# Sums of the expert outputs in three groups, other pages for expert weights, and the next block's first loads put last

## The chip, the cores and the metric

The kernel runs on one core of a Trainium2 chip. The metric is the device time of one execution in microseconds; three runs of the kernel before gave 3153.24, 3155.69 and 3157.79, median 3155.69. The core has a matrix engine (TensorE, PE in the rows, its weight loads PEld), VectorE (DVE), ScalarE (ACT), GpSimd (POOL) and SyncE (SP), which here issues nearly all DMAs from one queue, in order.

## The reference

Two transformer blocks over 512 tokens of width 1024, all in float32. The change lies in the mixture of experts of the first block and the entry of the second:

```
g_sel = argmax(x @ w_group + b_group)                 # 4 groups of 8 experts
e_top, e_loc = top_k(expert logits of the group, 2)   # 2 of 32 experts per token
hid = silu(xb @ w1[e]) * (xb @ w3[e])                 # 1024 -> 512, per expert e
ys  = hid @ w2[e]                                     # 512 -> 1024
out = segment_sum(ys * gate, token)                   # back to the tokens
h   = rmsnorm(h + g2 * out) * final_g
# block 2:
x   = layer_norm(h, ln_in_g, ln_in_b);  proj = x @ w_in[0]; ...
```

## The kernel before

**Expert stage.** The 32 experts are taken in 16 pairs; the two experts of a pair use 64 columns of TensorE's array each (`both`, L1368), so a matmul has tile `128*64`. Pair j does:

- `pair_in` (L1373): tokens times w1 and w3 of both experts. The weights come as 16 loads of 512 KB, each [128, 2, 512], and are used as float32 as they land (`w` in the rows, results `e`).
- `pair_tokens` (L1357): eight transposes (`xgt`) of the next pair's gathered tokens. `pair_gather` (L1354) is an indirect DMA from GpSimd, two pairs ahead.
- `pair_loads` and `pair_out` (L1390, L1400) for pair j-1: eight loads of 512 KB of w2 (`w2r`), four transposes of the hidden values (`hdt`), a copy (`hp`), then the matmuls.
- `outputs` (L1282): gate and scale (`y`), a split in two float32r parts (`yh`, `yl`), then eight sums over the tokens (`combine`, L1295). Each sum is two matmuls of tile `128*128` into a bank (`cmb`) and one addition into `h` on VectorE (L1303). `combine` is a generator, `beside`; the call of `pair_in` two pairs later advances it once after each of its eight pieces.

**What sets the order.** The code is written as dataflow on tiles; a scheduler with its own cost model puts the instructions of each engine in a fixed order, and an engine then keeps to it. A tile takes a page of its tag, and a load waits until the page's last reader is done: 24 pages PG (4 KB in each partition), 3 WH and 3 WL (4 KB), 3 RAW (8 KB), 3 banks for `trp`. In the pairs w1 and w3 use PG for their first two pieces, WH for the third, WL for the fourth; w2 uses PG. RAW, WH and WL are also used by `expert_in` and `expert_out` (L1318, L1333), inside a branch (`more`, L1423) for experts with more than 64 tokens. The branch's body does not run with these inputs, but a page that it uses is not loaded ahead of it for later use.

**Entry of block 2.** At j = 16 (L1460) three rows (`fgR`, `lng`, `lnb`, 512 KB each in the tile) and the first weights of block 2 (`nav_weights`, L1414: two RAW loads of 1024 KB, which `prepare` splits on ScalarE and VectorE into `wh`, `wl`) are asked for ahead of `pair_loads(15)`.

Of the kernel before, what the change touches and what calls it, by code (L numbers as in the profile page):

```python
# [10 lines left out]
F32 = mybir.dt.float32  # L11
# [53 lines left out]
def build(ctx, tc, I, out, dbg=None):  # L65
# [10 lines left out]
    def t_(shape, dt, tag, name):  # L76
        uid[0] += 1
        return sb.tile(shape, dt, tag=tag, bufs=NB[tag], name=f"{name}_{uid[0]}")
# [18 lines left out]
    def pipelined(n, score, out, steps=4):  # L97

        late = None
        for h in range(n + 1):
            for i in range(steps):
                if h < n:
                    score(h, i)
                if h:
                    products = out(h - 1, i)
                    rest = late and late()
                    late = products
                    if rest:  # L110
                        late = lambda a=rest, b=products: (a(), b())[1]
                yield
        while late:
            late = late()

    def sg(name, w=512, dt=F32):
        return t_([128, w], dt, "SG", name)
# [20 lines left out]
    def split(hi, lo, src, eng=None):  # L138
        S.copy(hi, src)  # L139
        (eng or V).tensor_tensor(lo, src, f(hi), OP.subtract)  # L140
# [144 lines left out]
    def mm3(ps, l, r, start, stop):  # L285

        mmk(ps, [(l, r)], start, stop)
# [35 lines left out]
    class FM:  # L323


        def __init__(self, W, xs, base, end, eng=None):
            self.eng = eng
            self.W, self.xs, self.base, self.end = W, xs, base, end
            self.kgs = groups(len(xs), 8)
            self.cur = -1  # L330
# [42 lines left out]
    class TM:  # L373
# [1 line left out]

        def __init__(self, kt, W, c0, n, name="tm", lead=0, tail=0):
            self.kt, self.W, self.c0, self.n, self.name, self.lead, self.tail = kt, W, c0, n, name, lead, tail
            gr = 2048 // n  # L380
            raws = [(k, min(gr, kt - k)) for k in range(0, kt, gr)] if n == 512 else groups(kt, gr)
            self.pieces = [(k0, k1, g1) for k0, g in raws for k1, g1 in groups(g, 1024 // n)]
            self.size = dict(raws)
            self.raw = {}
            for p in self.pieces[:lead]:
                self.fetch(p[0])
            self.first = None

        def fetch(self, k0):
            n, g = self.n, self.size[k0]  # L390
            if k0 not in self.raw:
                self.raw[k0] = t_([128, g, n], F32, "RAW", "raw")
                load(self.raw[k0], self.W[k0 * 128:(k0 + g) * 128, self.c0:self.c0 + n].rearrange("(k p) n -> p k n", p=128))
            return self.raw[k0]

        def piece(self, p, page=None):
# [580 lines left out]
    def row(name, src, pinned=False):  # L977
        t = pg(name, F32, (128, 1024))
        ins = load(t, src.partition_broadcast(128))
        if pinned:  # L980
            tc.keep_in_program_order(ins)
        return t
# [272 lines left out]
    def rows_of(t):  # L1255
        return lambda i: t[i * 128:(i + 1) * 128, :]
# [25 lines left out]
    def outputs(py, gtc, rows):  # L1282

        place = sa("place", 512, F32R)
        V.tensor_tensor(place.rearrange("p (i n) -> p i n", n=128), iota[:, 0:128].unsqueeze(1).to_broadcast([128, 4, 128]),
                        rows.unsqueeze(2).to_broadcast([128, 4, 128]), OP.is_equal)
        y = pt_("y", F32, (128, 1024))
        yh = pt_("yh", F32R, (128, 1024))
        yl = pt_("yl", F32R, (128, 1024))
        for m in range(2):  # L1290
            cs = slice(m * 512, m * 512 + 512)
            V.scalar_tensor_tensor(y[:, cs], py[m], gtc, g2R[:, cs], OP.mult, OP.mult)  # L1292
            split(yh[:, cs], yl[:, cs], y[:, cs])

        def combine():  # L1295
            for i in range(4):
                for m in range(2):
                    cs = slice(m * 512, m * 512 + 512)
                    ps = trp("cmb")
                    pl = place[:, i * 128:(i + 1) * 128]  # L1300
                    PE.matmul(ps, pl, yl[:, cs], start=True, stop=False)  # L1301
                    PE.matmul(ps, pl, yh[:, cs], start=False, stop=True)  # L1302
                    V.tensor_tensor(h1[i][m], h1[i][m], ps, OP.add)  # L1303
                    yield
        return combine()

    def tokens(tokc, xg):
        gather(tokc, xg)
# [9 lines left out]
    def expert_in(W1, W3, xh, xl):  # L1318
        pss = []
        for W in (W1, W3):  # L1320
            ps = mmp("e1")
            for q in range(4):
                raw = t_([128, 2, 512], F32, "RAW", "w13")
                load(raw, W[q * 256:(q + 1) * 256, :].rearrange("(k p) n -> p k n", p=128))
                hi = t_([128, 2, 512], F32R, "WH", "wh")
                lo = t_([128, 2, 512], F32R, "WL", "wl")
                split(hi, lo, raw)
                mmk(ps, [((xh[:, 2 * q + k], xl[:, 2 * q + k]), (hi[:, k], lo[:, k])) for k in range(2)],
                    q == 0, q == 3)
            pss.append(ps)  # L1330
        return hidden(*pss)

    def expert_out(hd, W2):  # L1333
        b = trp("hdt")
        for k in range(4):
            PE.transpose(b[:, k * 128:(k + 1) * 128], hd[:, k * 128:(k + 1) * 128], ident)
        hp = pt_("hp")
        split(hp[:, 0], hp[:, 1], b)
        py = [mmp("e2") for _ in range(2)]
        for k in range(4):  # L1340
            raw = t_([128, 1024], F32, "RAW", "w2r")
            load(raw, W2[k * 128:(k + 1) * 128, :])
            hi = t_([128, 1024], F32R, "WH", "wh")
            lo = t_([128, 1024], F32R, "WL", "wl")
            split(hi, lo, raw)
            for m in range(2):
                cs = slice(m * 512, m * 512 + 512)
                ks = slice(k * 128, k * 128 + 128)
                mm3(py[m], (hp[:, 0, ks], hp[:, 1, ks]), (hi[:, cs], lo[:, cs]), k == 0, k == 3)
        return py  # L1350


# [15 lines left out]
    def both(ps, lhs, rhs, start, stop):  # L1368
        for h in range(2):
            hs = slice(CAP * h, CAP * h + CAP)  # L1370
            PE.matmul(ps[hs], lhs[:, hs], rhs[h], start=start, stop=stop)  # L1371

    def pair_in(j, xT, beside):  # L1373
        pss = []
        for nm in ("moe_w1", "moe_w3"):
            W = [I[nm][0, 2 * j + h].rearrange("(p a) n -> p a n", a=8) for h in range(2)]
            ps = mmp("e1")
            for q in range(4):
                ws = []
                for h in range(2):  # L1380
                    raw = t_([128, 2, 512], F32, ("PG", "PG", "WH", "WL")[q], "w13")
                    load(raw, W[h][:, 2 * q:2 * q + 2])
                    ws.append(raw)
                for k in range(2):
                    both(ps, xT[:, 2 * q + k], [w[:, k] for w in ws], q + k == 0, q + k == 4)
                next(beside, None)
            pss.append(ps)
        return hidden(*pss)

# [10 lines left out]
    def pair_out(j, hd, ws):  # L1400
        b = trp("hdt")
        cols = hd.rearrange("p (a j) -> p j a", j=4)
        for k in range(4):
            PE.transpose(b[:, k * 128:(k + 1) * 128], cols[:, k], ident)
        hp = sg("hp")
        S.copy(hp, b)
        py = [mmp("e2") for _ in range(2)]
        for k in range(4):
            for m in range(2):
                cs = slice(m * 512, m * 512 + 512)  # L1410
                both(py[m], hp[:, k * 128:k * 128 + 128], [w[:, cs] for w in ws[2 * k:2 * k + 2]], k == 0, k == 3)
        return outputs(py, gt0[:, j:j + 1], rows0[:, :, j])

    def nav_weights(l):  # L1414
        return TM(8, I["w_in_2"][l], 1024, 512, "nav", lead=3)

    g2R = row("g2R", mod_d[3])
    xres = [dr.tile([512, 1024], F32, name=f"xres{n}") for n in range(4)]
# [24 lines left out]
    rows0 = const("rows0", [128, 4, 16])  # L1443
    token_rows(tok0, rows0)
    nav_tm = None
    beside = iter(())
    prev = None
    pair_gather(0)
    more(CAP)
# [2 lines left out]
    for j in range(17):  # L1452
        hd = None
        if j < 16:
            hd = pair_in(j, xs, beside)
        if j < 15:
            xs = pair_tokens(j + 1)
        if j < 14:
            pair_gather(j + 2)
        if j == 16:  # L1460
            fgR = row("fgR", I["final_g"])
            norm, xT = normalizer(I["ln_in_g_2"], I["ln_in_b_2"], rows_of(xres[0]))
            nav_tm = nav_weights(0).prepare()
        if prev is not None:
            for _ in beside:
                pass
            beside = pair_out(j - 1, prev, pair_loads(j - 1))
        prev = hd
    for _ in beside:
        pass  # L1470
# [507 lines left out]
```

## Time and profile before

| | |
|---|---|
| median of 3 runs | 3155.69 us |
| profiled execution | 3154.16 us, its span 3152.4 us |
| PE busy | 2970.1 us, 94% of the span |
| DVE / ACT / POOL busy | 1848.6 / 1131.5 / 279.6 us |
| HBM read | 486.50 MB |
| expert stage, first to last `e` matmul | 664.5 to 1205 us |

A row of the chain of waits is a piece of the path that ended last: start, length, engine, tile, line. A window row gives a stretch, the busy time of each engine, PE's granted clock (1.00 is full), the busy share of the 16 DMA engines and the GB/s that they moved. Times of rows are microseconds from the start of the span.

### The profile page before, as it was taken

To read this page: it belongs to the slowest core of one execution; us is meant where nothing else is said; L and a number is where in the kernel's file an instruction comes from. 1 tells how busy PE (TensorE), PEld (TensorE's weight loads), DVE (VectorE), ACT (ScalarE), POOL (GpSimd) and SP (SyncE) were. 2 spreads that over 40 slices of the span, in tenths; PEclk is the share of its full clock that TensorE was granted. 3 is DMA by queue.
4 is the path that set the end of the run, shared out by engine and by line. 5 is a ranking of instruction groups with operands and counts; after the bars stand their busy time and mean duration, and the time that the engine had idled before them with its cause. 6 is when DMAs were issued, how large, how long until landed. Compare 5 with 4: busy or idle time off the path is not lost.

```text
span 3152.4 us, 36476 instructions
## 1 busy us (share of the span) xinstructions
PE 2970.1 (94%) x13749; PEld 2204.3 (70%) x13749; DVE 1848.6 (59%) x3521; ACT 1131.5 (36%) x1986; POOL 279.6 (9%) x263
## 2 busy tenths in 40 slices
PE   6988999979999998999999999999999999999998
PEld 5766777733333335878867788888888876788887
DVE  6899888633223227555589754434545588764434
ACT  4555244210000003444567332222444576432221
POOL 2133000300000000221000200000221000200000
PEclk9989999989999999999999999999999999999999
DMA  6222756679999995432233623243433234632341
GB/s 222 92 90 65 233 185 195 208 289 353 362 372 377 358 376 193 137 114 94 76 112 111 231 100 107 92 142 100 147 117 101 79 99 116 225 107 93 107 139 62
DMA packets 296257, 534.17 MB, mean 169 GB/s; under 512 B 30279, under 2 KB 172789, under 8 KB 296071
## 3 DMA queue, kind: packets, MB, share of 16 engines
q1 hardware_dynamic: 293480, 527.46, 48.5%
q0 software_dynamic: 2304, 4.20, 0.5%
q8 instruction: 110, 1.80, 0.2%
q14 instruction: 77, 0.62, 0.1%
q10 hardware_dynamic: 286, 0.09, 0.0%
HBM read 486.50 MB, written 44.38 MB: 168 GB/s over the span
## 4 chain that ended last, share of the span: by engine, by line
PE 64%; DVE 7%; issue 3%; DMA 2%; ACT 2%; POOL 1%; SPq 0%; DVEq 0%; POOLq 0%; ACTq 0%
PE e L1371 12%; PE fm L292 9%; PE fm L295 9%; PE fm L293 9%; PE ffo L295 2%; PE ffo L293 2%; PE ffo L292 2%; PE cmb L1301 1%; PE cmb L1302 1%; POOL tl L1634 1%; DVE xT L140 1%; DMA w2r<-in_moe_w_dram 1%; PE mix L292 1%; PE mix L295 1%; PE mix L293 1%
## 5 line engine op out<-in xcount | busy, mean ns | idle before, releaser
L140 DVE TENSOR_TENSOR wl<-raw,wh 128x1024 fp32r<-128x1024 f32 (+3 forms) x403 | 462.3, 1149 | 313.8 <-ACT wh L139 312.2
L139 ACT CAST wh<-raw 128x1024 fp32r<-128x1024 f32 (+3 forms) x403 | 388.6, 966 | 543.0 <-PE fm L295 224.2
L292 PE MATMUL fm<-xT,wh 128*128 128x512 f32 (+1 forms) x1264 | 481.9, 384 | 0.0
L293 PE MATMUL fm<-xT,wl 128*128 128x512 f32 (+1 forms) x1264 | 479.9, 382 | 1.3 <-DVE wl L140 1.3
L295 PE MATMUL fm<-xT,wh 128*128 128x512 f32 (+1 forms) x1264 | 301.9, 381 | 0.0
L1371 PE MATMUL e<-w,xx 128*64 128x512 f32 x1024 | 293.8, 605 | 0.0
L293 PEld LDWEIGHTS fm<-xT,wl 128*128 128x128 f32 x1264 | 238.2, 188 | 46.7 <-DVE wl L140 1.7
L292 PEld LDWEIGHTS fm<-xT,wh 128*128 128x128 f32 x1264 | 238.2, 189 | 45.1
L295 PEld LDWEIGHTS fm<-xT,wh 128*128 128x128 f32 x1264 | 231.6, 188 | 45.5
L1371 PEld LDWEIGHTS e<-w,xx 128*64 128x64 f32 x1024 | 79.2, 137 | 138.6 <-issue 130.0
L293 PE MATMUL fm<-uT,wl 128*128 128x512 f32 (+1 forms) x360 | 145.3, 403 | 3.8 <-DVE wl L140 3.8
L1303 DVE TENSOR_TENSOR h<-h,cmb 128x512 f32<-128x512 f32 x128 | 84.6, 686 | 109.2 <-PE cmb L1302 108.5
L1371 PE MATMUL e<-w2r,hp 128*64 128x512 f32 x512 | 141.9, 607 | 3.6 <-DMA w2r<-in_moe_w_dram 2.1
L292 PE MATMUL fm<-uT,wh 128*128 128x512 f32 (+1 forms) x360 | 145.0, 404 | 0.0
L292 PE MATMUL ffo<-wl,hid 128*128 128x512 f32 x352 | 137.1, 390 | 0.0
L293 PE MATMUL ffo<-wh,hid 128*128 128x512 f32 x352 | 136.9, 389 | 0.0
L1371 PEld LDWEIGHTS e<-w2r,hp 128*64 128x64 f32 x512 | 52.8, 137 | 87.9 <-issue 64.5
L1921 DVE SCALAR_TENSOR_TENSOR ffs<-ffs,fm 128x512 f32<-128x512 f32 x44 | 30.3, 688 | 137.7 <-ACT ffs L1920 137.7
L295 PE MATMUL ffo<-wh,hid 128*128 128x512 f32 x352 | 108.4, 389 | 0.0
L139 ACT CAST yh<-y 128x512 fp32r<-128x512 f32 x32 | 19.8, 618 | 224.2 <-DVE y L1292 224.2
L1923 DVE SCALAR_TENSOR_TENSOR ffs<-ffs,fm 128x512 f32<-128x512 f32 x44 | 30.3, 688 | 114.4 <-PE fm L295 114.4
L1634 POOL TENSOR_TENSOR tl<-ml,tl 128x512 f32<-128x512 f32 x32 | 47.7, 1497 | 554.3 <-DVE tl L1630 540.6
(603 smaller groups left out, 5955.6 us busy)
## 6 DMA issues: line engine op xcount, KB each, us to landing
w<-in_moe_w_dram SPq DMA_DIRECT2D x256, 512.0 KB
raw<-in_w_in_dram SPq DMA_DIRECT2D x71, 1024.0 KB
w2r<-in_moe_w_dram SPq DMA_DIRECT2D x128, 512.0 KB
raw<-in_w_ffn_in_dram SPq DMA_DIRECT2D x44, 1024.0 KB
raw<-in_w_mod_dram SPq DMA_DIRECT2D x42, 512.0 KB
raw<-in_w_ffn_out_dram SPq DMA_DIRECT2D x20, 1024.0 KB
raw<-in_w_out_dram SPq DMA_DIRECT2D x12, 1024.0 KB
t_d<-bg SPq DMA_DIRECT2D x48, 256.0 KB
```

The lines of the kernel that those rows point to most:

```text
L139: S.copy(hi, src)
L140: (eng or V).tensor_tensor(lo, src, f(hi), OP.subtract)
L292: PE.matmul(ps, l[0], r[1], start=start and n == 0, stop=False)
L293: PE.matmul(ps, l[1], r[0], start=False, stop=False)
L295: PE.matmul(ps, l[0], r[0], start=False, stop=stop and n == len(pairs) - 1)
L1301: PE.matmul(ps, pl, yl[:, cs], start=True, stop=False)
L1302: PE.matmul(ps, pl, yh[:, cs], start=False, stop=True)
L1303: V.tensor_tensor(h1[i][m], h1[i][m], ps, OP.add)
L1371: PE.matmul(ps[hs], lhs[:, hs], rhs[h], start=start, stop=stop)
L1634: G.tensor_tensor(th, m, th, OP.add)
L1921: V.scalar_tensor_tensor(s, s, 1.0, pgt, OP.add, OP.mult)
L1923: V.scalar_tensor_tensor(s, s, 0.5, pup, OP.mult, OP.mult)
```

## The change

- `behind(ins, first)` makes an instruction stand behind another of its engine. `pair_in` hands the last matmul of a piece to `combine`, and the first sum of a group is put behind it. The eight sums come in groups of 3, 3 and 2 instead of one per piece.
- The pieces of w1 are 4, 2 and 2 long on RAW, PG, PG; of w3 2, 2, 2, 2 on PG, PG, WH, WL. So a pair has two loads of 1024 KB (8 KB in a row of HBM) and twelve of 512 KB for w1 and w3.
- `expert_in` and `expert_out` take their weights in halves through small pages (`sg`, `sa`) and no longer use RAW.
- At j = 16 the rows and the first weights of block 2 are asked for behind `pair_loads(15)`, kept in program order, and `prepare` is called behind `pair_out`.

```diff
+    def behind(ins, first):
+        tc.add_manual_dep(ins.ins, first.ins.name, mybir.DependencyInfo(mybir.DependencyClass.NoSync, mybir.DependencyReason.DATA),
+                          reason="order")
+        return ins
...
         def combine():
+            after = yield
             for i in range(4):
                 for m in range(2):
...
-                    PE.matmul(ps, pl, yl[:, cs], start=True, stop=False)
+                    mm = PE.matmul(ps, pl, yl[:, cs], start=True, stop=False)
+                    if after is not None:
+                        behind(mm, after)
                     PE.matmul(ps, pl, yh[:, cs], start=False, stop=True)
                     V.tensor_tensor(h1[i][m], h1[i][m], ps, OP.add)
-                    yield
+                    after = yield
...
-            for q in range(4):
+            k = 0
+            for tag, w, banks in ((("RAW", 4, 0), ("PG", 2, 3), ("PG", 2, 0)), (("PG", 2, 3), ("PG", 2, 0), ("WH", 2, 2), ("WL", 2, 0)))[n]:
                 ws = []
                 for h in range(2):
-                    raw = t_([128, 2, 512], F32, ("PG", "PG", "WH", "WL")[q], "w13")
-                    load(raw, W[h][:, 2 * q:2 * q + 2])
+                    raw = t_([128, w, 512], F32, tag, "w13")
+                    load(raw, W[h][:, k:k + w])
                     ws.append(raw)
-                for k in range(2):
-                    both(ps, xT[:, 2 * q + k], [w[:, k] for w in ws], q + k == 0, q + k == 4)
-                next(beside, None)
+                for m in range(w):
+                    mm = both(ps, xT[:, k + m], [r[:, m] for r in ws], k + m == 0, k + m == 7)
+                k += w
+                if beside:
+                    for b in range(banks):
+                        try:
+                            beside.send(None if b else mm)
+                        except StopIteration:
+                            pass
...
-        if j == 16:
-            fgR = row("fgR", I["final_g"])
-            norm, xT = normalizer(I["ln_in_g_2"], I["ln_in_b_2"], rows_of(xres[0]))
-            nav_tm = nav_weights(0).prepare()
...
-            beside = pair_out(j - 1, prev, pair_loads(j - 1))
+            ws = pair_loads(j - 1)
+            if j == 16:
+                fgR = row("fgR", I["final_g"], True)
+                norm, xT = normalizer(I["ln_in_g_2"], I["ln_in_b_2"], rows_of(xres[0]))
+                nav_tm = nav_weights(0, True)
+            beside = pair_out(j - 1, prev, ws)
+            if j == 16:
+                nav_tm.prepare()
```

TensorE's order at the end of w2 and the start of a later pair's w1, in a middle pair, before (`e` with `w` are w1 and w3, `cmb` the sums; the trace records two matmuls for each `e` row):

```order
L1371 MATMUL e_1487_7324<-w_1488_7325,xx_7256 64x512
L1301 MATMUL cmb_7333<-yl_7317,place_7313 128x512
L1302 MATMUL cmb_7333<-yh_7316,place_7313 128x512
L1301 MATMUL cmb_7345<-yl_7317,place_7313 128x512
L1371 MATMUL e_1487_7324<-w_1489_7327,xx_7256 64x512
L1371 MATMUL e_1487_7324<-w_1488_7325,xx_7256 64x512
L1371 MATMUL e_1487_7324<-w_1489_7327,xx_7256 64x512
L1302 MATMUL cmb_7345<-yh_7316,place_7313 128x512
L1301 MATMUL cmb_7357<-yl_7317,place_7313 128x512
L1302 MATMUL cmb_7357<-yh_7316,place_7313 128x512
```

The same place now, from the last of the twelve `e` rows that stand between w2 and the first group:

```order
L1385 MATMUL e_1527_7500<-w_1531_7515,xx_7432 64x512
L1311 MATMUL cmb_7521<-yl_7493,place_7489 128x512
L1314 MATMUL cmb_7521<-yh_7492,place_7489 128x512
L1311 MATMUL cmb_7525<-yl_7493,place_7489 128x512
L1314 MATMUL cmb_7525<-yh_7492,place_7489 128x512
L1311 MATMUL cmb_7529<-yl_7493,place_7489 128x512
L1314 MATMUL cmb_7529<-yh_7492,place_7489 128x512
L1385 MATMUL e_1527_7500<-w_1535_7533,xx_7432 64x512
```

The sums stood in six small runs, beginning one `e` row behind w2; now they stand in three, with 12, 4 + 4 and 8 `e` rows ahead of them. With the transposes, a pair had eight runs of tile `128*128` (3, 3, 3, 3, 3 sum matmuls; 1 with 3 `xgt`; 5 `xgt` with 1 `hdt`; 3 `hdt`) and has five (6, 6, 4 sum matmuls; 5 `xgt`; 3 `xgt` with all 4 `hdt`, directly ahead of w2).

SP's order where the expert weights begin, ahead of the branch, before:

```order
L979 DMA g2R_5623<-mod_d 128x1024
L1382 DMA w_1336_6761<-in_moe_w_dram 128x1024
L1382 DMA w_1337_6763<-in_moe_w_dram 128x1024
L1382 DMA w_1338_6769<-in_moe_w_dram 128x1024
L1382 DMA w_1339_6771<-in_moe_w_dram 128x1024
L1382 DMA w_1345_6794<-in_moe_w_dram 128x1024
L1382 DMA w_1346_6796<-in_moe_w_dram 128x1024
```

and now:

```order
L988 DMA g2R_5623<-mod_d 128x1024
L1399 DMA w_1384_6953<-in_moe_w_dram 128x2048
L1399 DMA w_1386_6965<-in_moe_w_dram 128x1024
L1399 DMA w_1387_6967<-in_moe_w_dram 128x1024
L1399 DMA w_1388_6973<-in_moe_w_dram 128x1024
L1399 DMA w_1389_6975<-in_moe_w_dram 128x1024
L1399 DMA w_1391_6982<-in_moe_w_dram 128x1024
L1399 DMA w_1385_6955<-in_moe_w_dram 128x2048
```

Ahead of the branch stood 16 loads of w1 and w3 and four of w2, all of 512 KB; now the same number of these and three RAW loads of 1024 KB among them, the third two rows ahead of the first store of the tokens (`u_d`, L1063 before).

VectorE's order at the last sums (`h<-h,cmb`) and the first row of block 2 (`fgR`), now:

```order
L1315 TENSOR_TENSOR h_964_4973<-h_964_4973,cmb_9603 128x512
L146 TENSOR_TENSOR wl_9568<-raw_9527,wh_9567 128x1024
L146 TENSOR_TENSOR wl_9572<-raw_9527,wh_9571 128x1024
L1315 TENSOR_TENSOR h_964_4973<-h_964_4973,cmb_9607 128x512
L146 TENSOR_TENSOR wl_9576<-raw_9529,wh_9575 128x1024
L1965 TENSOR_TENSOR h_961_4964<-h_961_4964,fgR_9521 128x1024
```

Before, the three `wl` of block 2's first weights stand ahead of `y` of the last pair; now they are among its last sums. From `fgR` on, all engines' orders are the same as before.

## Rows read from the trace of the kernel before

**Rows 1.** Page: DMA issues with KB each, and the indirect gathers' queue (packets, MB, share)
```profile
q0 software_dynamic: 2304, 4.20, 0.5%
...
w<-in_moe_w_dram SPq DMA_DIRECT2D x256, 512.0 KB
...
w2r<-in_moe_w_dram SPq DMA_DIRECT2D x128, 512.0 KB
```

**Rows 2.** Windows: stretch, length, busy time per engine, PEclk, DMA share, GB/s
```profile
937.00:958.00 21.00, 20.00 (x70) 7.33 (x67) 7.82 (x12) 1.24 (x2) 0.00 (x0) 1.00 1.02 410
961.00:970.00 9.00, 9.00 (x44) 3.37 (x45) 1.38 (x2) 1.73 (x3) 0.99 (x1) 1.00 0.88 315
605.00:620.00 15.00, 15.00 (x68) 12.40 (x67) 10.61 (x20) 2.74 (x4) 6.86 (x5) 1.00 0.24 82
686.00:1166.00 480.00, 465.15 (x1740) 172.06 (x1736) 147.12 (x218) 41.60 (x70) 11.94 (x12) 1.00 0.96 367
1180.00:1203.00 23.00, 19.24 (x64) 7.62 (x63) 11.24 (x15) 4.66 (x6) 0.00 (x0) 0.93 1.03 401
```

**Rows 3.** Chain of waits over one middle pair: start, length, what
```profile
929.62 15.43 PE e L1371 x64
...
945.86 0.63 ACT yh L139
...
947.75 1.86 PE e L1371 x6
949.61 0.43 PE cmb L1302
950.03 0.23 PE cmb L1301
...
950.50 1.00 PE e L1371 x2
...
960.67 0.76 PE xgt L1364 x5
...
963.41 0.56 PE hdt L1404 x3
963.96 1.43 PE e L1371 x5
```

**Rows 4.** Waits of SP's queue, 660 to 1210 us: total us, times, longest
```profile
SPq L1382 <- PE e L1371: 166.9, 35, 8.7
```

**Rows 5.** Timeline of SP and DVE: start, length, engine, what
```profile
610.67 1.23 DVE L140 TENSOR_TENSOR wl<-raw,wh 128x1024 fp32r<-128x1024 f32 x1 [1.35 <-ACT wh L139]
...
622.09 0.33 SPq L1063 DMA_DIRECT2D u_d<-u  x1
...
662.73 2.85 SPq L1382 DMA_DIRECT2D w<-in_moe_w_dram  x6
```

**Rows 6.** Chain of waits at the first w2 of the stage
```profile
697.91 0.60 ACT hp L1406
...
698.55 6.65 PE e L1371 x29
```

**Rows 7.** Timeline of the last two pairs and block 2's entry
```profile
1176.27 9.55 PE L1371 MATMUL e<-w2r,hp 128*64 128x512 f32 x31
...
1178.76 1.63 SPq L393 DMA_DIRECT2D raw<-in_w_in_dram  x2
...
1185.00 1.61 DVE L1292 SCALAR_TENSOR_TENSOR y<-e,gts,g2R 128x512 f32<-128x512 f32 x2 [7.41 <-PE e L1371]
...
1194.29 3.50 DVE L140 TENSOR_TENSOR wl<-raw,wh 128x1024 fp32r<-128x1024 f32 x3 [1.21 <-ACT wh L139]
...
1194.82 10.86 PE L1371 MATMUL e<-w2r,hp 128*64 128x512 f32 x32 [2.13 <-DMA w2r<-in_moe_w_dram]
...
1204.86 1.61 DVE L1292 SCALAR_TENSOR_TENSOR y<-e,gts,g2R 128x512 f32<-128x512 f32 x2 [7.08 <-PE e L1371]
...
1212.94 1.22 DVE L1939 TENSOR_TENSOR h<-h,fgR 128x1024 f32<-128x1024 f32 x1
```

More of the change, by code (lines that the diff above doesn't have):

```diff
@@ L373, in build, with __init__ @@
     class TM:
-        def __init__(self, kt, W, c0, n, name="tm", lead=0, tail=0):
+        def __init__(self, kt, W, c0, n, name="tm", lead=0, tail=0, pinned=False):
+            self.pinned = pinned
             self.kt, self.W, self.c0, self.n, self.name, self.lead, self.tail = kt, W, c0, n, name, lead, tail
@@ L392, in fetch @@
                 self.raw[k0] = t_([128, g, n], F32, "RAW", "raw")
-                load(self.raw[k0], self.W[k0 * 128:(k0 + g) * 128, self.c0:self.c0 + n].rearrange("(k p) n -> p k n", p=128))
+                ins = load(self.raw[k0], self.W[k0 * 128:(k0 + g) * 128, self.c0:self.c0 + n].rearrange("(k p) n -> p k n", p=128))
+                if self.pinned:
+                    tc.keep_in_program_order(ins)
             return self.raw[k0]
@@ L1300, in combine @@
                     pl = place[:, i * 128:(i + 1) * 128]
-                    PE.matmul(ps, pl, yl[:, cs], start=True, stop=False)
+                    mm = PE.matmul(ps, pl, yl[:, cs], start=True, stop=False)
+                    if after is not None:
+                        behind(mm, after)
                     PE.matmul(ps, pl, yh[:, cs], start=False, stop=True)
                     V.tensor_tensor(h1[i][m], h1[i][m], ps, OP.add)
-                    yield
-        return combine()
+                    after = yield
+        sums = combine()
+        next(sums)
+        return sums
     def tokens(tokc, xg):
@@ L1322, in expert_in @@
             for q in range(4):
-                raw = t_([128, 2, 512], F32, "RAW", "w13")
-                load(raw, W[q * 256:(q + 1) * 256, :].rearrange("(k p) n -> p k n", p=128))
                 hi = t_([128, 2, 512], F32R, "WH", "wh")
                 lo = t_([128, 2, 512], F32R, "WL", "wl")
-                split(hi, lo, raw)
+                for k in range(2):
+                    raw = sg("w13")
+                    load(raw, W[(2 * q + k) * 128:(2 * q + k + 1) * 128, :])
+                    split(hi[:, k], lo[:, k], raw)
                 mmk(ps, [((xh[:, 2 * q + k], xl[:, 2 * q + k]), (hi[:, k], lo[:, k])) for k in range(2)],
@@ L1340, in expert_out @@
         for k in range(4):
[L1341 to L1345, printed above, removed]
+            ks = slice(k * 128, k * 128 + 128)
+            hi = t_([128, 2, 512], F32R, "WH", "wh")
+            lo = t_([128, 2, 512], F32R, "WL", "wl")
             for m in range(2):
-                cs = slice(m * 512, m * 512 + 512)
-                ks = slice(k * 128, k * 128 + 128)
-                mm3(py[m], (hp[:, 0, ks], hp[:, 1, ks]), (hi[:, cs], lo[:, cs]), k == 0, k == 3)
+                raw = sa("w2r")
+                load(raw, W2[ks, m * 512:m * 512 + 512])
+                split(hi[:, m], lo[:, m], raw)
+                mm3(py[m], (hp[:, 0, ks], hp[:, 1, ks]), (hi[:, m], lo[:, m]), k == 0, k == 3)
         return py
@@ L1370, in both @@
             hs = slice(CAP * h, CAP * h + CAP)
-            PE.matmul(ps[hs], lhs[:, hs], rhs[h], start=start, stop=stop)
+            mm = PE.matmul(ps[hs], lhs[:, hs], rhs[h], start=start, stop=stop)
+        return mm
     def pair_in(j, xT, beside):
         pss = []
-        for nm in ("moe_w1", "moe_w3"):
+        for n, nm in enumerate(("moe_w1", "moe_w3")):
             W = [I[nm][0, 2 * j + h].rearrange("(p a) n -> p a n", a=8) for h in range(2)]
             ps = mmp("e1")
-            for q in range(4):
+            k = 0
+            for tag, w, banks in ((("RAW", 4, 0), ("PG", 2, 3), ("PG", 2, 0)), (("PG", 2, 3), ("PG", 2, 0), ("WH", 2, 2), ("WL", 2, 0)))[n]:
                 ws = []
                 for h in range(2):
-                    raw = t_([128, 2, 512], F32, ("PG", "PG", "WH", "WL")[q], "w13")
-                    load(raw, W[h][:, 2 * q:2 * q + 2])
+                    raw = t_([128, w, 512], F32, tag, "w13")
+                    load(raw, W[h][:, k:k + w])
                     ws.append(raw)
-                for k in range(2):
-                    both(ps, xT[:, 2 * q + k], [w[:, k] for w in ws], q + k == 0, q + k == 4)
-                next(beside, None)
+                for m in range(w):
[7 more added lines that the diff above has]
+                            pass
             pss.append(ps)
@@ L1412, in pair_out, with nav_weights @@
         return outputs(py, gt0[:, j:j + 1], rows0[:, :, j])
-    def nav_weights(l):
-        return TM(8, I["w_in_2"][l], 1024, 512, "nav", lead=3)
+    def nav_weights(l, pinned=False):
+        return TM(8, I["w_in_2"][l], 1024, 512, "nav", lead=3, pinned=pinned)
     g2R = row("g2R", mod_d[3])
@@ L1445, in build @@
     nav_tm = None
-    beside = iter(())
+    beside = None
     prev = None
@@ L1459, in build @@
             pair_gather(j + 2)
-        if j == 16:
-            fgR = row("fgR", I["final_g"])
-            norm, xT = normalizer(I["ln_in_g_2"], I["ln_in_b_2"], rows_of(xres[0]))
-            nav_tm = nav_weights(0).prepare()
         if prev is not None:
-            for _ in beside:
+            for _ in beside or ():
                 pass
-            beside = pair_out(j - 1, prev, pair_loads(j - 1))
+            ws = pair_loads(j - 1)
[6 more added lines that the diff above has]
+                nav_tm.prepare()
         prev = hd
```

## The prediction, made before the changed kernel ran

> **What bounds the kernel now.** The windows over the expert stage come first [rows 2]: from 686 to 1166 us TensorE is at full clock and busy, and the DMA engines are at a share of 0.96 and 367 GB/s. So two resources are near their end in one stage, and the question is which of them has slack. The finer windows answer for DMA: in the 21 us from 937 it runs at a share of 1.02 and 410 GB/s, and in the 9 us from 961 it falls to 0.88 and 315. Each pair has such a dip. The waits of SP's queue name its cause: 35 waits, 166.9 us in all and up to 8.7 us long, of a weight load for a matmul of the expert stage to let go of its page [rows 4]; behind each stands all the rest of SP's one queue.
>
> The chain of waits over one pair shows what TensorE does [rows 3]. The long run of w3 and w2 begins at 929.62 and again at 963.96: a cycle is 34.3 us. It is nearly all TensorE: 64 matmuls in 15.43 us, then small pieces, runs of six in 1.86 and of two in 1.00, each followed by sums or transposes of the other tile. From these two lengths a matmul takes (1.86 - 1.00) / 4 = 0.215 us, and a run costs 1.00 - 2 x 0.215 = 0.57 on top of its matmuls. The first sum matmul of a run takes 0.43, a further one 0.23. The 64 should take 64 x 0.215 + 0.57 = 14.33; the 1.1 more are waits for w2 loads. And ahead of the next run, at 947.75, the chain leaves TensorE for y, yh (945.86) and yl, since the first sums stand one row behind w2.
>
> **The change part by part.** First the cycle of TensorE in a middle pair, from w2 of one pair to w2 of the next, by the new order. There are 96 matmuls of the experts as before, in runs of 56, 16, 16, 2 and 6: 96 x 0.215 + 5 x 0.57 = 23.5 us. Sums: two runs of six, each 0.43 + 5 x 0.235 = 1.60, and one of four, 1.13: 4.3. Transposes: five xgt 0.76 [rows 3], and seven (3 xgt, 4 hdt) at 0.56 for three and 0.1 for each more, 0.96. New is that all hdt stand directly ahead of w2, so the copy hp lies open: 0.60 and two short gaps, 0.7 in all [rows 6]. The wait for y, yh and yl falls away, because 12 rows, 5 us of matmuls, now stand ahead of the first group. Sum: 23.5 + 4.3 + 0.8 + 1.0 + 0.7 = 30.2 us, against 34.3. The waits added by the explicit order hold only an instruction that stands there in any case; behind it wait the next matmuls, and nobody waits for a sum before the end of the stage. The three banks are free again for a next group after three additions, about 2 us, which 8 rows (3.4 us) cover.
>
> Now the loads. A pair has 24 loads of 512 KB before (384 in 16 pairs [rows 1]), 12.58 MB; at 410 GB/s that is 30.7 us. A gather holds the engines 0.5% x 3152 / 16 = 1.0 us [rows 1]. So loads need 31.7 us in a cycle, if pages don't stop them. Do they? Before, a pair wants four of the three WH pages and four of three WL, so SP stops in the middle of the pair. Now it wants two RAW of three, two WH of three, two WL of three, and 16 PG of some 20 (24 less two for gathered tokens, one for g2R, one for constants). The pages for a whole next w1 and w3, 8.4 MB or 20 us of loading, are free when the pair's own w1 and w3 are done. I take the dips as gone, and the share as that of the better windows.
>
> What no row shows is a load with 8 KB in a row of HBM, a sixth of the bytes. The nearest rows are the 1024 KB loads of block 2 within 1180 to 1203, where everything moved at 401 GB/s [rows 2], and 410 for the 512 KB ones; the ends are 315 and something above 410, and I take 410. With 315 for that part a cycle takes 1.5 us longer, 33.2.
>
> The start. Three RAW loads, 3.1 MB, come ahead of the branch. Their pages come free when the last splits of w_out are done, the third at 611.9 [rows 5]. DMA has room there: its share is 0.24 from 605 to 620 [rows 2], and the first store of the tokens only comes at 622.09, so I cost this at nothing; without that cover it would be 3.1 MB / 410 = 7.7 us on the way to the router. By then 13.6 MB instead of 10.5 are on the chip. The first two pairs' w1 and w3 contain no sums; TensorE begins the first w2 at 698.55 [rows 6], and I leave that, though the loads will be ahead.
>
> The end of w1 and w3 of the last pair is at 1176.3 before [rows 7], 14 cycles after the first w2. For TensorE: 698.6 + 14 x 30.2 = 1121. For the loads: by then 16 x 8.39 + 14 x 4.19 MB are needed, less 13.6 on the chip: 179.3 MB, 437 us, with 14 gathers 451, from 662.7, where SP resumes after the branch [rows 5], and 2 us for the first to land: 1116. The two are so near that they will not overlap wholly: waits for loads cost TensorE 1.1 us a cycle before; I take 0.4 of it, 6 us. So 1127 instead of 1176.3.
>
> The tail. Before, w2 of pair 14 follows until y at 1185.0, then its sums and the last transposes, and w2 of pair 15 waits 2.13 us for its loads, which stand in SP's queue behind three rows and two 1024 KB loads, and runs 10.86 us instead of 32 x 0.215 + 0.57 = 7.4 [rows 7]; y of the last pair is at 1204.9. Now w2(15) comes ahead of those 3.6 MB. TensorE alone: 1127 + 7.4, then 8.4 (1185.0 to 1194.82 less 2.13 of waiting, plus 0.7 for hp), then 7.4: 1150. The loads: last w2 bytes at 1116 + 8.39 MB / 410 = 1137, in time. So y comes 54 us earlier. Against it: the three splits wl of block 2's weights, 3.50 us of VectorE [rows 7], were done while TensorE waited for the last loads; now they stand among the last sums, ahead of fgR. Their loads land near 1137 + 3.6 MB / 410 = 1146 and 2 us, in time, so the splits cost their own 3.5 us and no more. From fgR on nothing is moved.
>
> Sum: 54 - 3.5 = 50 us off the profiled execution's 3154.2: 3104; that execution lies 1.5 us below the median, so 3105 as a median.
>
> **The rivals.** First, the loads do not go faster: 367 GB/s is what HBM gives this core on average, and the dips belong to the gathers. Then 179.3 MB and 14 gathers' 3.7 MB take 499 us, w1 and w3 of pair 15 end at 1164, the last w2 bytes land at 1187, y follows at 1188: 17 earlier, less 3.5 for the splits: a median of 3142. Against it stands the 21 us long window at 410, with the dip beginning exactly where SP stops. In the Trainium skill, "DMA: Bandwidth & Descriptors", section "Where 436 GB/s comes from", the HBM side is said to bind a core's loads at about 358 GB/s. By that figure the stage would gain nothing, and the time, an estimate from that page, would be near 3152; this case's windows at 410 disagree with it.
>
> Second, TensorE's cycle shrinks less than the runs say: say the first sum, the transposes and w2 each wait 0.7 us more, as hp does, 2 us a cycle, 28 us in all: 3133. For it: the order now has fewer matmuls between an hdt and its use. Against: sums and copies lie behind 3 to 5 us of matmuls.
>
> Third, slower: the 8 KB rows load badly. A cycle's other 10.5 MB take 25.6 us and a gather 1.0; the two RAW loads, 2.1 MB, then decide. TensorE cannot begin a pair's w1 without them. At 280 GB/s they take 7.5 us and the cycle is the old 34.1 ((1176.3 - 698.6) / 14). The tail would still give some 4 us, so the kernel is slower by 6 us from 258 GB/s downwards; at 240 the cycle is 35.4, 14 of them lose 18, and with the tail 14 remain: 3170. The lowest mean in the rows is 315, in a dip that is a lack of issues, not a slow load; so this is unlikely.
>
> That the change does not do what it says is excluded by the built order: three groups, the splits and the queue stand as described.
>
> **How the numbers follow.** The forecast 0.87, with its own range 3092 (no meeting waits, splits hidden, the first w2 earlier by a few us) to 3122 (1.1 us of waits a cycle and 8 KB rows a little slower). The first rival 0.04, the second 0.06, the third or no change 0.03. The second lies just beyond the forecast's own range; I take 3092 to 3130, which leaves out about 0.15. What a measurement can tell from no change is 0.2%, 6 us; only the third rival and small remnants of the first fall there or above: faster 0.95, same 0.03, slower 0.02.
>
> **What would show it.** The distance of two pairs' hdt near 31 us; runs of e of 56, 16 and 16; no idle stretch of TensorE ahead of the first sum; SP's waits for e far below 166.9 us; a DMA share of 1.0 and above 395 GB/s over the stage; the last y near 1150 and fgR near 1162. Wrong would be a cycle above 33 us, with either DMA at 1.0 and below 380 GB/s (first or third rival, told apart by the landing of the RAW loads), or DMA still dipping and TensorE waiting.

## The result, and the profile after

The changed kernel takes 3099.22 us (median of 4 runs, 3094.82 to 3100.77) where the one before took 3154.61 in the same session: ratio 0.9821, 95% interval 0.9804 to 0.9838. Measured again beside other kernels it was 3098.98, ratio 0.9816 (0.9802 to 0.9830). The forecast was 3105, with 3092 to 3130 as its range: 50 us of gain were worked out, 55 came.

The profiled execution spans 3098.6 us. The windows over the expert stage answer [rows 2], in the same columns:

```profile
686.00:1106.00 420.00, 399.66 (x1720) 158.67 (x1718) 137.02 (x211) 41.80 (x70) 11.86 (x12) 1.00 1.02 410
937.00:958.00 21.00, 19.20 (x82) 7.20 (x81) 6.05 (x10) 2.40 (x4) 0.99 (x1) 1.00 1.02 408
605.00:620.00 15.00, 15.00 (x67) 12.37 (x67) 10.61 (x19) 3.60 (x4) 8.22 (x5) 1.00 0.90 338
```

What was the rate of the better windows before, 410 GB/s at a share of 1.02, is now that of the whole stage. The dips are gone. The last row is the stretch ahead of the stage that had room: the RAW loads fill it.

SP's waits from 660 to 1150 us show the same from the queue's side (total, times, longest):

```profile
SPq L1399 <- DMA w<-in_moe_w_dram: 117.9, 84, 3.2
SPq L1419 <- DMA w<-in_moe_w_dram: 104.1, 112, 2.4
SPq L1399 <- DMA w2r<-in_moe_w_dram: 96.8, 104, 2.1
SPq L1399 <- PE e L1385: 22.0, 36, 4.3
```

The wait for a page that a matmul holds fell from 166.9 to 22.0 us [rows 4]. SP now waits for earlier loads in its own queue, that is, for DMA itself.

The chain of waits over a middle pair (start, length, what) answers [rows 3]:

```profile
902.65 13.27 DMA w<-in_moe_w_dram
...
915.97 5.36 PE e L1385 x22
921.33 0.43 PE cmb L1311
...
922.93 3.58 PE e L1385 x16
...
928.11 3.58 PE e L1385 x16
...
932.84 1.00 PE e L1385 x2
933.84 0.75 PE xgt L1378 x5
934.59 1.86 PE e L1385 x6
936.45 0.53 PE xgt L1378 x3
936.98 0.50 PE hdt L1427 x4
...
937.50 0.59 ACT hp L1429
...
938.14 3.39 PE e L1385 x15
941.53 14.76 DMA w<-in_moe_w_dram
...
956.31 10.20 DMA w2r<-in_moe_w_dram
```

From 915.97 to 966.51 half of it, 25.0 of 50.5 us, is loads now, and no y, yh or yl stands in it. From one hdt to the next the timeline of TensorE gives the cycles: hdt begins at 697.63, 725.46, 753.32, 782.38, 811.45, 842.26, 873.80, 905.58 and 936.82. So the cycle is 27.8 for the first two pairs, 29.1 for the next two, then 30.8 and 31.2 to 31.8; the longest, later, is 32.2 (hdt at 968.55 and 1000.74). For the first four, TensorE goes at its own pace on what is already on the chip; after that DMA sets it.

The timeline of the tail answers [rows 7]:

```profile
1130.10 1.61 DVE L1301 SCALAR_TENSOR_TENSOR y<-e,gts,g2R 128x512 f32<-128x512 f32 x2 [5.58 <-PE e L1385]
...
1138.46 7.09 PE L1385 MATMUL e<-w2r,hp 128*64 128x512 f32 x32 [0.68 <-ACT hp L1429]
...
1144.76 1.58 DVE L1301 SCALAR_TENSOR_TENSOR y<-e,gts,g2R 128x512 f32<-128x512 f32 x2 [6.59 <-PE e L1385]
...
1152.20 2.35 DVE L146 TENSOR_TENSOR wl<-raw,wh 128x1024 fp32r<-128x1024 f32 x2
...
1156.20 1.22 DVE L1965 TENSOR_TENSOR h<-h,fgR 128x1024 f32<-128x1024 f32 x1
```

w2 of the last pair waits for hp only, and takes 7.1 instead of 10.9 us. The last y is 60.1 us earlier than before, fgR 56.7: the splits wl stand ahead of it. This execution came to the stage 2.2 us later (u_d at 624.32 instead of 622.09 [rows 5]; g2R, ahead of the first expert load, is already 2.3 us later), so the stage itself won more than the kernel shows.

### The profile page after: what moved, and what is told of

The parts are those of the page before. It is cut to its first block, busy times and chain, and to the rows that moved or that the text cites. A ratio compares the mean times of both kernels' runs of the same rounds, so it can differ in the third digit from the quotient of the medians.

```text
span 3098.6 us, 36572 instructions
## 1 busy us (share of the span) xinstructions
PE 2908.0 (94%) x13749; PEld 2192.0 (71%) x13749; DVE 1840.3 (59%) x3521; ACT 1131.2 (37%) x1986; POOL 279.1 (9%) x263
## 4 chain that ended last, share of the span: by engine, by line
PE 57%; DMA 10%; DVE 6%; issue 3%; ACT 2%; POOL 1%; SPq 0%; DVEq 0%; POOLq 0%; ACTq 0%
PE fm L298 9%; PE fm L301 9%; PE fm L299 9%; DMA w<-in_moe_w_dram 6%; PE e L1385 5%; DMA w2r<-in_moe_w_dram 3%; PE ffo L301 2%; PE ffo L298 2%; PE ffo L299 2%; PE mix L298 1%; PE mix L299 1%; PE mix L301 1%; POOL tl L1660 1%; DVE wl L146 1%; PE cmb L1311 1%
## 5 line engine op out<-in xcount | busy, mean ns | idle before, releaser
L1385 PE MATMUL e<-w,xx 128*64 128x512 f32 x1024 | 256.8, 600 | 10.9 <-DMA w<-in_moe_w_dram 10.9
L1385 PE MATMUL e<-w2r,hp 128*64 128x512 f32 x512 | 115.1, 596 | 10.1 <-ACT hp L1429 10.1
L1947 DVE SCALAR_TENSOR_TENSOR ffs<-ffs,fm 128x512 f32<-128x512 f32 x44 | 30.2, 687 | 139.3 <-ACT ffs L1946 139.3
L1949 DVE SCALAR_TENSOR_TENSOR ffs<-ffs,fm 128x512 f32<-128x512 f32 x44 | 30.2, 687 | 114.4 <-PE fm L301 114.4
L1946 ACT ACTIVATE ffs<-fm 128x512 f32<-128x512 f32 x44 | 26.3, 598 | 188.7 <-PE fm L301 188.7
L1385 PEld LDWEIGHTS e<-w2r,hp 128*64 128x64 f32 x512 | 41.1, 136 | 73.1 <-issue 58.9
```

The lines of the kernel that those rows point to most:

```text
L1385: mm = PE.matmul(ps[hs], lhs[:, hs], rhs[h], start=start, stop=stop)
L1946: S.activation(s, pgt, AF.Tanh, scale=0.5)
L1947: V.scalar_tensor_tensor(s, s, 1.0, pgt, OP.add, OP.mult)
L1949: V.scalar_tensor_tensor(s, s, 0.5, pup, OP.mult, OP.mult)
```

## The experiments

Eleven runs were made, each timed beside the kernel before on the same chip; one (e0) is the second measurement of the changed kernel given above. Ratios are to the kernel before.

**The sums alone** (e1): before with `combine`, `behind` and `both` of the change, and this in `pair_in`, the four page kinds as before:

```diff
-                next(beside, None)
+                if beside:
+                    for b in range(((0, 0, 3, 0), (3, 0, 2, 0))[n][q]):
+                        try:
+                            beside.send(None if b else mm)
+                        except StopIteration:
+                            pass
```

> The kernel before with the new grouping and explicit order of the sums alone; pages of w1 and w3 and the tail as before. Theory (two resources meet): TensorE's own cycle falls to about 28 us, as the first cycles of the changed kernel show (697.63 to 725.46), but SP still waits for WH and WL pages inside a pair, so the loads need 31.2 us and a smaller dip: cycle 32 to 33, 14 cycles save 15 to 29 us, time 3125 to 3140, and SP's waits for a matmul of the experts still over 60 us. Rival (the grouping alone is the gain): cycle 31.2 or below, time near 3100 to 3105. Rival (the pages alone are the gain): nothing moves, 3150 to 3155.

Measured: 3112.11 us, ratio 0.9852 (0.9837 to 0.9867). That is 46 us, more than the theory gave. Two middle hdt are at 912.43 and 943.78, 31.35 apart. The stretch from 686 to 1106 and SP's waits over the stage:

```profile
686.00:1106.00 420.00, 406.79 (x1680) 162.07 (x1677) 134.22 (x207) 40.67 (x68) 11.87 (x12) 1.00 1.02 404
```
```profile
SPq L1394 <- PE e L1382: 77.1, 35, 5.7
```

The pages are the old ones, the number of stops is the old one (35), but they are half as long in all, and with DMA at a share of 1.02 the loads already issued bridge most of them. So the dips before were not made by the pages alone: they were as long as they were because TensorE gave its pages back late. The forecast's step from page counts to "SP stops" had the place right and the dependence on TensorE missing.

**The pages alone** (e2): before with the loads of w1 and w3 in RAW (4 rows), PG, WH and WL as in the change; one bank of sums behind each two rows:

```diff
+            for tag, w in ((("RAW", 4), ("PG", 2), ("PG", 2)), (("PG", 2), ("PG", 2), ("WH", 2), ("WL", 2)))[n]:
...
+                    if m % 2:
+                        next(beside, None)
```

> The kernel before with the new pages of w1, w3 (and of the loop that doesn't run) alone; one sum bank behind each two rows as before, tail as before. Theory: the loads could go at 31.2 us a cycle, but TensorE keeps its small runs and its wait for y, yh, yl: its cycle without load waits is 34.3 less 1.1 = 33.2, so 14 cycles save about 12 us: 3138 to 3147, with SP's waits for a matmul far below 166.9 us in number or moved to where TensorE is late. Rival (the pages alone are the gain): 3100 to 3110. Rival (the sums alone): 3150 to 3155.

Measured: 3124.23, ratio 0.9887 (0.9872 to 0.9903): 34 us, not the 12 expected. Here TensorE sets the cycle: hdt at 913.79 and 946.38, 32.6 apart, and its weight loads waited for w only 5.7 us in all 16 pairs. SP nevertheless stands for matmuls as long as before, where it was 166.9 us [rows 4]:

```profile
SPq L1383 <- PE e L1371: 162.2, 50, 9.8
```

With new pages and a late TensorE the stops stay; with old pages and an early one (e1) they halve. What TensorE loses here is in its timeline (bracket: idle before, and for what):

```profile
920.86 7.45 PE L1371 MATMUL e<-w2r,hp 128*64 128x512 f32 x31
930.15 0.47 PE L1301 MATMUL cmb<-yl,place 128*128 128x512 f32 x1 [1.84 <-DVE yl L140]
```

The wait for yl is 1.56 and 1.84 us in two cycles. TensorE's own cycle is 32.5 instead of the 33.2 worked out, and one more early cycle is short: the third takes 28.5 (hdt at 752.77 and 781.31) instead of 35.0.

The pages are not alone in this kernel. With other pages the scheduler also put the sums in other places: behind the wait for yl the runs of `e` in this cycle are 2, 22, 2, 6 and 2, so that a pair has six runs instead of eight. At 0.57 each, two runs fewer are 1.1 us a cycle, enough for the step from 33.2 to 32.5. How much of the 34 us the pages alone would give is not shown; what they add to the sums is seen below, in e4 against e1.

Neither edit is the whole gain. The sums bring TensorE below what the loads need, some 31.4 us even with the old pages. Without them TensorE stays the limit at 32.5, and the pages can only take away its waits for loads.

**The late loads of block 2 alone** (e3): before, with fgR, lng, lnb and the first weights issued behind `pair_loads` of the last pair.

```diff
-        if j == 16:
-            fgR = row("fgR", I["final_g"])
...
+            ws = pair_loads(j - 1)
+            if j == 16:
+                fgR = row("fgR", I["final_g"], True)
...
+                nav_tm = nav_weights(0, True)
+            beside = pair_out(j - 1, prev, ws)
```

> The kernel before with only rows and first weights of block 2 loaded last. Theory: w2 of the last pair no longer waits (2.13 us ahead of it and 10.86 less 7.1 within it), 5.9 us; the three splits wl now lie ahead of fgR, 3.4 us back: 3150 to 3155, not to be told from before, or just. Rival (the late loads are a large part of the gain): below 3145.

Measured: 3157.34, ratio 0.9993 (0.9984 to 1.0002). As expected, no difference that can be told.

**All but the late loads** (e4): the changed kernel with this part undone.

```diff
-            ws = pair_loads(j - 1)
-            if j == 16:
-                fgR = row("fgR", I["final_g"], True)
...
+        if j == 16:
+            fgR = row("fgR", I["final_g"])
...
+            beside = pair_out(j - 1, prev, pair_loads(j - 1))
```

> The changed kernel with rows and first weights of block 2 loaded where they were before. Theory: the last w2 loads come 3.6 MB later, 8.8 us, but w2 of the last pair starts only at 1138.46 in the changed kernel, some 7 us behind its loads, so little of this is seen; the splits wl lie beside the loads again and give 3.4 us back: 3096 to 3103, the same as the changed kernel's 3099.2 or a little less. Rival (the late loads are needed once the stage is bound by loads): 8 us slower than the changed kernel, 3105 to 3110.

Measured: 3096.05, ratio 0.9804 (0.9790 to 0.9817). This overlaps the changed kernel's 0.9816 and 0.9821. The late loads have no gain that can be told here either. Where they pay and where they cost is seen when the tail is cut by its milestones, in us:

```
                     last w3 to last y   last y to fgR   fgR to first nav matmul
before                       29.4              7.2               7.5
late loads alone             24.5             10.6               8.4
all but late loads           27.3              7.2               7.5
changed kernel               22.4             10.6               8.5
```

They give 4.9 us on the way to y and take back 3.4 for the splits and 1.0 behind fgR. The hdt tell what the pages add to the sums (from e1's 0.9852 to 0.9804): with the sums alone the first cycle is 27.8 and the second 31.0 already, with both it is 29.1 or less for four. The first six cycles are 185.1 us in e1 and 175.3 here, the next eight 248.2 and 247.5. The pages give a lead, not a faster middle.

**Fewer bytes** (e6): four of the rows of w1 are loaded for the first expert of a pair only and used for both.

```diff
-                for h in range(2):
+                for h in range(1 if w == 4 else 2):
...
+                if w == 4:
+                    ws.append(ws[0])
```

> The changed kernel with one load of 1024 KB less for each pair (the first four rows of w1 of the second expert of a pair are left out, those of the first taken for both), so 11.5 instead of 12.6 MB a pair; every matmul stays. Theory (loads at 410 GB/s are the limit now, TensorE's own cycle is 27.9 us): loads want 28.1 + 0.5 = 28.6 us, the cycle falls from 31.2 to 28 to 29, waits for w nearly go, 25 to 33 us less than the changed kernel: 3066 to 3076. Rival (TensorE's cycle is the 30.2 us of the forecast): the cycle falls by 1 us at most, 3085 to 3095. Rival (pages, not bytes, bound the loads): no change.

Measured: 3071.95, ratio 0.9731 (0.9717 to 0.9744); 27 us below the changed kernel on the same chip. TensorE's matmuls no longer wait for w (10.9 us in the changed kernel), its weight loads only in pieces of at most 0.4 us (17.5 us in all; there 20.6, up to 2.4), and it runs through:

```profile
952.45 0.65 PE L1429 MATMUL hdt<-ident,hid 128*128 128x128 f32 x4
953.77 7.14 PE L1385 MATMUL e<-w2r,hp 128*64 128x512 f32 x32 [0.68 <-ACT hp L1431]
960.69 5.37 PE L1385 MATMUL e<-w,xx 128*64 128x512 f32 x24
965.99 0.50 PE L1311 MATMUL cmb<-yl,place 128*128 128x512 f32 x1
```

Its cycle stays at 29.07 (hdt at 923.39, 952.45, 981.52). So 29.1 is TensorE's own cycle in a middle pair, and bytes were what held it at 31.2. Pages were not: SP stands for matmuls 53.6 us here, longer than the 24.2 of the changed kernel. The saved 1.05 MB would be 2.6 us a cycle; only 2.1 are seen, since TensorE is met on the way.

**Less work for TensorE** (e5): the matmul of the low half of each sum is left out, eight a pair; loads and additions stay.

```diff
-                    mm = PE.matmul(ps, pl, yl[:, cs], start=True, stop=False)
+                    mm = PE.matmul(ps, pl, yh[:, cs], start=True, stop=True)
...
-                    PE.matmul(ps, pl, yh[:, cs], start=False, stop=True)
```

> The changed kernel with the low half of each sum left out (one matmul a bank instead of two; yl is still written): TensorE's cycle is eight matmuls, 1.9 us, shorter, every load and every addition stays. Theory (loads are the limit from the sixth pair on): the middle cycle stays at 31.2 us, the first ones go from 27.9 to 26 and only use up the lead of the loads sooner: 3096 to 3100, within 3 us of the changed kernel's 3099. Rival (TensorE's cycle is the limit, as the forecast's 30.2 says for it plus waits): 14 cycles at 1.9 us, 20 to 27 us less: 3072 to 3080.

Measured: 3097.94, ratio 0.9811 (0.9798 to 0.9825): no change. The first cycles fall to 26.0 and 27.1, and the fourth is 31.2 already (hdt at 775.86, 807.08, 838.30). What TensorE saves, it waits.

**A longer lead** (e9): the loop that doesn't run is moved off WH and WL too, so that six more loads of pairs 0 and 1 stand ahead of the branch.

```diff
-                hi = t_([128, 2, 512], F32R, "WH", "wh")
-                lo = t_([128, 2, 512], F32R, "WL", "wl")
...
+                    hi, lo = sa("wh", dt=F32R), sa("wl", dt=F32R)
```

> The changed kernel with the loop that doesn't run moved off the WH and WL pages as well (its weights are split in small pages): six more loads of 512 KB of pairs 0 and 1 stand ahead of the branch in SP's queue, in the time from 640 to 665 us in which SP stood. Theory (bytes at 410 GB/s from 665 us on are the limit): 3.1 MB less after the branch, 7.7 us, seen whole at the end, since TensorE's own cycle has room: 3090 to 3093. Rival (the lead is used up by TensorE's first cycles and lost): no change, 3097 to 3101. Slower, if the loads that now wait for the last matmuls of w_out hold the stores of the tokens behind them: the first matmul of the experts later than 665, above 3101.

Measured: 3098.79, ratio 0.9807 (0.9793 to 0.9820). The rival holds; the theory's sum of bytes from 665 us on was wrong. SP's timeline tells why. First the changed kernel (e0), then this one:

```profile
663.18 7.35 SPq L1399 DMA_DIRECT2D w<-in_moe_w_dram  x7
671.92 2.52 SPq L1419 DMA_DIRECT2D w2r<-in_moe_w_dram  x4
678.78 18.87 SPq L1399 DMA_DIRECT2D w<-in_moe_w_dram  x16
```
```profile
669.82 0.34 SPq L1396 DMA_DIRECT2D w<-in_moe_w_dram  x1
671.54 2.52 SPq L1416 DMA_DIRECT2D w2r<-in_moe_w_dram  x4
678.40 19.46 SPq L1396 DMA_DIRECT2D w<-in_moe_w_dram  x16
```

The seven loads fall to one, but the next sixteen start at the same time, since all pages are full and only the first pair's matmuls free them: from 640 to 700 us SP waits 23.8 us in four waits of w for such matmuls, against 13.9 in five in the changed kernel. The lead is a number of pages, not of microseconds.

The same edit on the kernel of e4, so with the late loads undone (e10):

> As the one before with the six loads ahead of the branch, and rows and first weights of block 2 loaded where they were before the change. Theory: the loads of the last w2 come 7.7 us sooner than in the changed kernel without the late loads, where TensorE waited 1.83 us ahead of them and 3.8 us within; the splits wl stay beside the loads: 3087 to 3091, some 2 to 4 us below the one before. Rival (the late loads of block 2 are worth something): above the one before.

Measured: 3100.28, ratio 0.9812 (0.9798 to 0.9825). No gain either.

**The last sums among the last w2** (e7): `pair_out` of the last pair sends three, three and two banks of pair 14's sums behind its rows 1, 2 and 3.

```diff
-            for _ in beside or ():
-                pass
+            if j < 16:
+                for _ in beside or ():
+                    pass
...
+            if sums:
+                for s in range((0, 3, 3, 2)[k]):
+                    try:
+                        sums.send(None if s else mm)
```

> The changed kernel with the sums of pair 14 put in groups of 3, 3 and 2 between the rows of the last pair's w2, instead of ahead of it. Theory: TensorE no longer stands for y, yl and the eight sums of pair 14 (1130.10 to 1137.04) ahead of hdt of pair 15; its loads have landed by about 1131.5, so w2 of the last pair starts some 5 to 6 us earlier and gets 16 sum matmuls of 4 us into it, whose additions lie beside it: y of the last pair 2 to 5 us earlier, fgR too: 3094 to 3098, 2 to 5 us below the changed kernel. Rival (the tail is bound by the last loads): no change.

Measured: 3097.69, ratio 0.9806 (0.9792 to 0.9819), no difference. w2 of the last pair does start early, but its sums end no sooner: the two halves of y now come 2.5 us apart, with TensorE standing 1.54 and 1.38 us for yl and busy for only 2.08 of the 5 us ahead of 1145. Behind that the granted clock of the stretch 1145 to 1151 is 0.52, the 1.2 GHz level, with TensorE busy throughout; in the changed kernel it is 1.00 in its last sums (second block):

```profile
1145.00:1151.00 6.00, 5.95 (x14) 4.13 (x13) 4.25 (x7) 4.29 (x6) 0.00 (x0) 0.52 0.06 20
```
```profile
1147.00:1152.00 5.00, 4.74 (x16) 2.53 (x16) 4.77 (x8) 2.62 (x4) 0.00 (x0) 1.00 0.12 41
```

**And block 2's first splits on GpSimd** (e8), on the kernel of e7:

```diff
-            split(hi, lo, raw[:, k1:k1 + g1, :])
+            split(hi, lo, raw[:, k1:k1 + g1, :], G if self.pinned else None)
```

> As the one with the last sums among w2, and the splits wl of block 2's first weights on GpSimd instead of VectorE. A split wl of 128 x 1024 takes 2.5 us there in the trace, three 7.6 us, and the first matmul that needs them comes 10 us after the loads landed. Theory: fgR no longer stands behind 3.4 us of VectorE's splits: 3 to 4 us below the one before, 3090 to 3095. Rival: what fgR wins, the first matmuls of block 2 lose by waiting for GpSimd: no change.

Measured: 3101.24, ratio 0.9820 (0.9807 to 0.9834). fgR comes at 31.5 us behind the last w3 instead of 34.7 in e7, as expected, but this step itself takes 3.03 instead of 1.21 us, and block 2 takes the rest back: from its first nav matmul to its first ffs it is 620.6 instead of 616.5 us. Why was not followed.

None of these is measurably below the changed kernel, but for the one that leaves bytes out.

## Why the prediction came out

**The bound.** Two resources near their end, and the loads held by pages: right in both, and the share and rate it named (1.0, above 395 GB/s) are those of the profile. But "dips by pages" was taken as a property of the pages. e1 shows that with the old pages and an earlier TensorE the rate is 404, and e2 that with the new pages and a late TensorE SP still stands 162.2 us.

**TensorE's cycle**, 30.2 predicted, measured 29.07 (e6). The term that was mis-sized is the 0.57 for each of five runs, 2.85 us. Two runs of 16 take 3.58, 16 x 0.215 + 0.14, and the run of 56 in e6 (953.77 to 965.99) 12.22, 56 x 0.215 + 0.18; only the runs of 2 and 6 carry 0.57 and 0.57. Together 1.6: 1.25 less, and 30.2 becomes 28.95. The price had been read off runs of 2 and 6 [rows 3] and was charged to runs of another kind.

What tells the kinds apart is not the neighbour but the number of `e` rows. A row is two recorded matmuls, so 2, 6 and 22 are odd numbers of rows, and 8, 16 and 56 even ones. A run of 8 next to transposes in the changed kernel is cheap, 8 x 0.215 + 0.15, and a run of 22 between sums in e2 is dear, 22 x 0.215 + 0.56, as are the runs of 6 and 2 between sums in [rows 3]:

```profile
722.67 1.87 PE e L1385 x8
724.53 1.09 PE xgt L1378 x8
```
```profile
934.76 5.29 PE e L1371 x22
940.06 0.43 PE cmb L1301
```

The difference, some 0.43, is the time of one more row. `both` sends the rows to the two halves of the array in turn, so an odd run leaves one row without its partner; this fits the runs shown here but was not tested by itself. Before, all eight runs of a middle pair were odd (66 with the row ahead of the first sum, then 6, 2, 6, 2, 6, 2 and 6), now two of five are. By these prices that is 8 x 0.57 less 1.6, an estimated 3.0 of the 5.2 us between 34.3 and 29.07. In the first two pairs the 2 and 6 stand as one run of 8, and the cycle is 27.8. hp, 0.7, was right: TensorE's matmuls wait 10.1 us for it in 15 pairs.

**The loads' cycle**, 31.7 predicted, measured 31.2 in the shortest cycles from the sixth on and 31.6 in the mean of the seven from 842.26 to 1063.19. 24 loads and a gather are 12.85 MB, 31.3 us at the stage's 410 GB/s, so the gather costs about its bytes, 0.6, and not 1.0. With a sixth of the bytes in 8 KB rows the rate is 410 GB/s, the value taken; the third rival's 258 is excluded.

**The start**, put at nothing, was right: from g2R to the first u_d it is 34.0 us in the kernel before and 33.9 in the changed one (32.3 to 35.1 in the other kernels with the three RAW loads ahead of it).

**The two together.** 1127 was worked out for the end of w1 and w3 of the last pair, 428 us behind the first w2; it is 1123.2 and 424. The forecast compared two ends, 1121 for TensorE and 1116 for the loads, and so named TensorE. In the middle that is wrong: there TensorE waits at the first piece of each pair, 1.1 to 1.5 us, which two ends don't show, and e5 and e6 settle that bytes set the cycle. Only the last cycle is TensorE's own again: the last w is issued at 1108.9, and it takes 27.5 us. With 28.95 in the forecast's own sum TensorE's end would be 698.6 + 14 x 28.95 = 1104, the loads' 1116 the later one, and with the same 6 us 1122, 423 us behind the first w2. So the wrong limit was named, and it is luck that this cost only 5 us: the mis-sized term put TensorE's end 17 us late, next to that of the loads.

**The tail.** w2 of the last pair: 8.36 us from y of pair 14 (8.4 predicted), and 7.1 long (7.4). From the last y to fgR 11.44 against 8.08 + 3.5. All as worked out; the last y is 60.1 us earlier instead of 54 mainly because the stage before it ended earlier. "From fgR on nothing is moved" missed 1.0: two of the three small VectorE steps (`rst`) of the first row block take 0.69 and 0.64 us instead of 0.16. At fgR 56.7 us are won, at the end 53.8; the rest, 2 us, lies in block 2, whose length from the first nav matmul to the first ffs varies from 614.5 to 617.3 us in these kernels without any edit there. That part was not followed further.

**The rivals.** HBM as the limit at 367 GB/s is refuted by 410 GB/s over 420 us. In the Trainium skill, "DMA: Bandwidth & Descriptors", section "Where 436 GB/s comes from", the HBM side is put at about 358 GB/s a core, half of what the two cores of a stack share, and is said to bind. This kernel runs on one core, and its 410 GB/s show that it does not bind here. Worked as the first rival was, this figure of the Trainium skill gives an estimate of 3155, not the 3152 put down. That the sums' grouping alone gives most is something no rival had: e1 gives 46 us, the whole change 55.

## What to carry to other kernels

When two resources both stand near the cycle, ask which of them holds the other up: a queue that stops for pages may be waiting only because the pages' user is late, and making that user faster starts the queue again. Then the gains of two edits don't add (46 and 34 us alone, 62 together). To see which limit is left, take away bytes in one kernel and work in another, and believe the one that moves. An edit of pages can also change the order that a scheduler builds, so compare the order before calling an experiment one part of a change. And a price read off short runs holds for runs of their kind only.

## What was not expected of the hardware

One core's loads ran at 408 to 410 GB/s at a DMA share of 1.02 for over 400 us, with gathers between them and rows of HBM of 4 and 8 KB mixed.

A run of matmuls with 64 columns each costs 0.14 to 0.18 us on top of 0.215 a matmul when its number of `e` rows is even, and 0.56 to 0.57 when it is odd, next to sums as well as to transposes (8, 16 and 56 against 2, 6 and 22 recorded matmuls).

In seven of the eight profiles with late loads (not in e8), two of the three small VectorE steps that follow fgR take 0.50 to 0.71 us instead of 0.16; in the kernels without late loads, before, e1, e2, e4 and e10, they take 0.16. What makes them slow was not found.
